# A two-layer block with a product-key expert choice on one core: which engine adds the candidate scores

## The chip, the cores and the metric

The kernel runs on one core of a Trainium2 chip. A core has five engines, each with its own queue of instructions: TensorE (PE in the rows; PEld is its weight load), VectorE (DVE), ScalarE (ACT), GpSimd (POOL) and SyncE (SP), which here only issues DMAs. The engines wait for each other by semaphores. The metric is the time of one execution in microseconds of device time, as the median of several runs. A profiled execution gives the start and the length of each instruction.

## The reference, cut to what matters

The program computes two transformer blocks over 512 tokens of width 1024, in float32. The second ends in `peer`: for each token and each of 8 heads two lists of 128 key scores are made, the best 16 of either list are taken, all sums of one of the first and one of the second list are formed, and the best 16 sums name 16 of 16,384 experts.

```python
def chunk(xc):
    q = (xc @ wq).reshape(PEER_CHUNK, PEER_HEADS, 2, half)
    s1 = jnp.einsum('chd,hnd->chn', q[:, :, 0], keys1).astype(jnp.float32)
    s2 = jnp.einsum('chd,hnd->chn', q[:, :, 1], keys2).astype(jnp.float32)
    v1, i1 = lax.top_k(s1, PEER_TOPK)
    v2, i2 = lax.top_k(s2, PEER_TOPK)
    cand = (v1[..., :, None] + v2[..., None, :]).reshape(PEER_CHUNK, PEER_HEADS, PEER_TOPK * PEER_TOPK)
    cidx = (i1[..., :, None] * PEER_N_KEYS + i2[..., None, :]).reshape(PEER_CHUNK, PEER_HEADS, PEER_TOPK * PEER_TOPK)
    best, pos = lax.top_k(cand, PEER_TOPK)
    eidx = jnp.take_along_axis(cidx, pos, axis=-1)
    g = jax.nn.softmax(best, axis=-1)
    a = jnp.einsum('chkd,cd->chk', u_tab[eidx], xc)
    wgt = (jax.nn.gelu(a.astype(jnp.float32)) * g).astype(xc.dtype)
    return jnp.einsum('chk,chkd->cd', wgt, v_tab[eidx])
```

## The kernel before

The first block, its mixture of experts and the second block's attention and convolution run up to about 1370 us. Then `peer` (L1395) begins. Its 512 tokens are four tiles of 128. Three tiles get their experts by dense products over the whole tables, with a weight of nought for what wasn't chosen; the fourth gathers its rows one by one with indirect DMAs. `peer` has three stages: the key choice (about 1380 to 1629 us), the making of the weight matrix from the choice (`gs`, to about 1930 us), and the products with the second table.

**The key choice** is a loop over 8 heads (L1604 to L1611). In each round the scores of the next head are made first and the present head's choice after them:

- `scores(h)` (L1522), for either half: a weight of 512 KB is loaded (`wraw`) and split into an upper part `whi` by ScalarE (L69) and a lower part `wlo` by GpSimd (L70); TensorE makes 24 products of 512 columns in three kinds (L87 to L89) into a bank `acc`; ScalarE copies it to `pq` (L1534); TensorE multiplies it with the keys (L1538); ScalarE copies the scores to `sk` (L1540). VectorE's `top16` (L1385) then takes the best 16 of each of the four tiles: a search for 8 values (L1388), their places (L1389), a copy without them (L1391), a second search (L1392) and its places (L1393), into `tkv` and `tki`.
- `best16(h)` (L1546): four instructions (L1551) add the two lists into `cand`, 80 sums per tile, those of the 256 that can be among the best 16. Three of them write 64 elements per partition, one 128. VectorE's `top16` looks for the best 16 sums (`best`, `pos`). ScalarE makes exponentials of them (`gslot`, L1565, with a load of its table in front). VectorE computes from `pos` which entries of the two lists make a sum (L1576 to L1582); ScalarE casts the result (`pu`, L1587), and VectorE looks the key numbers up (`eq`, L1590 to L1597, and `e`, L1598). ScalarE copies them to `slot` (L1599) and `ei` (L1602).

Beside it runs work of the later stages. `ahead` (L1436) makes chunks of the dense first product, each with a weight of its own (`whi`, `wlo`, 24 products of 384 columns, a gelu into `ga` at L1430, which needs another table in ScalarE): one after each half, one more in odd heads. `gather(2)` (L1478) starts two indirect DMAs of GpSimd in each head from head 1 on (`grow`, L1493); from head 2 on it multiplies a row gathered earlier with the token (L1503, GpSimd), and ScalarE sums it up (L1504).

**What sets the order.** The program is built under a scheduler that reorders the instructions of an engine by times of its own, within their dependencies. GpSimd is taken out of that from L1474 on: there its order is that of the code. So a head of GpSimd's queue is: four or five `wlo`, the four sums, the row products. TensorE, VectorE, ScalarE and SyncE are in the scheduler's order. TensorE has two `acc` banks and starts a group when ScalarE has copied the group before the last.

In `best16`, `tt` is VectorE's `tensor_tensor` (L1398). The blocks of the sums are (first place in `cand`, first entry of list one, its entries, entries of list two):

```python
BLOCKS = ((0, 0, 2, 16), (32, 2, 2, 8), (48, 4, 4, 4), (64, 8, 8, 2))
```

Of the kernel before, what the change touches and what calls it, by code (L numbers as in the profile page):

```python
# [46 lines left out]
class Emit:  # L47
# [1347 lines left out]
    def peer(self):  # L1395
        tc, nc, A = self.tc, self.nc, self.A
        mm = nc.tensor.matmul
        tt, ts, stt = nc.vector.tensor_tensor, nc.vector.tensor_scalar, nc.vector.scalar_tensor_tensor  # L1398
# [6 lines left out]
        with ExitStack() as es:  # L1405
# [30 lines left out]
            def ahead(n, eng=nc.gpsimd):  # L1436
                for _ in range(n):
                    if nu[0] < AHEAD:
                        u_chunk(nu[0], eng)
                        nu[0] += 1  # L1440
# [73 lines left out]
            with ExitStack() as ek:  # L1514
# [31 lines left out]
                def best16(h, val, ixu):  # L1546


                    cand = pk.tile([128, NT, 80], F32, name="cand")
                    for o, i0, ni, nj in BLOCKS:  # L1550
                        nc.gpsimd.tensor_tensor(  # L1551
                            cand[:, :, o:o + ni * nj].rearrange("p t (i j) -> p t i j", i=ni),
                            val[:, :, 0, i0:i0 + ni, None].to_broadcast([128, NT, ni, nj]),
                            val[:, :, 1, None, 0:nj].to_broadcast([128, NT, ni, nj]), op=ALU.add)
                    best = pk.tile([128, NT, 16], F32, name="best")
                    pos = pk.tile([128, NT, 16], U32, name="pos")
                    for t in range(NT):
                        self.top16(pk, cand[:, t], 80, best[:, t], pos[:, t])
                    ahead(h % 2)
                    g = pk.tile([128, NT, 16], F32, name="gslot")  # L1560
                    mx = pk.tile([128, NT], F32, name="bmx")
                    nm = pk.tile([128, NT], F32, name="bnm")
                    nc.scalar.activation(nm, best[:, :, 0], AF.Copy, scale=-1.0)
                    for t in range(NT):
                        nc.scalar.activation(g[:, t], best[:, t], AF.Exp, bias=nm[:, t:t + 1],  # L1565
                                             accum_out=mx[:, t:t + 1])
                    nc.vector.reciprocal(mx, mx)
                    hs = slice(h * 16, h * 16 + 16)
                    tt(slot[:, 2, :, hs], g[:, :ND], mx[:, :ND, None].to_broadcast([128, ND, 16]), op=ALU.mult)
                    tt(gg[:, hs], g[:, ND], mx[:, ND:NT].to_broadcast([128, 16]), op=ALU.mult)  # L1570
                    kf = pk.tile([128, NT, 2, 16], F16, name="kfl")
                    nc.scalar.activation(kf, ixu, AF.Copy)


                    u = [pk.tile([128, NT, 16], U32, name=f"pu{i}", bufs=1) for i in range(3)]
                    ts(u[0], pos, 2, 0x3c, op0=ALU.logical_shift_left, op1=ALU.bitwise_and)  # L1576
                    ts(u[0], u[0], 0x40, None, op0=ALU.bitwise_or)
                    ts(u[1], pos, 4, 7, op0=ALU.logical_shift_right, op1=ALU.bitwise_xor)
                    tt(u[2], u[0], u[1], op=ALU.logical_shift_right)
                    tt(u[1], u[2], u[1], op=ALU.logical_shift_left)  # L1580
                    tt(u[0], u[0], u[1], op=ALU.bitwise_xor)
                    ts(u[0], u[0], 0x3c, None, op0=ALU.bitwise_and)  # L1582
                    e = pk.tile([128, 2, NT, 16], F32, name="e12")
                    for half in range(2):

                        pu = pk.tile([128, NT * 16, 2], F16, name=f"pu2{half}")
                        nc.scalar.activation(pu, (u[0] if half else u[2]).rearrange("p t k -> p (t k)")[:, :, None]  # L1587
                                             .to_broadcast([128, NT * 16, 2]), AF.Copy)
                        eq = pk.tile([128, NT * 16, 16], F16, name="eq", bufs=2)
                        tt(eq.rearrange("p n (i j) -> p n i j", j=2), pu[:, :, None].to_broadcast([128, NT * 16, 8, 2]),  # L1590
                           i16[:, half].rearrange("p (i j) -> p i j", j=2)[:, None].to_broadcast([128, NT * 16, 8, 2]),
                           op=ALU.is_equal)
                        eq4 = eq.rearrange("p (t k) i -> p t k i", t=NT)
                        tt(eq4, eq4, kf[:, :, half, None, :].to_broadcast([128, NT, 16, 16]), op=ALU.mult)

                        for n in (8, 4):
                            tt(eq[:, :, 0:n], eq[:, :, 0:n], eq[:, :, n:2 * n], op=ALU.add)  # L1597
                        red(e[:, half].rearrange("p t k -> p (t k)"), eq[:, :, 0:4], axis=AX.X, op=ALU.add)  # L1598
                    nc.scalar.activation(slot[:, 0:2, :, hs], e[:, :, :ND], AF.Copy)  # L1599
                    ef = pk.tile([128, 16], F32, name="ef")  # L1600
                    stt(ef, e[:, 0, ND], 128.0, e[:, 1, ND], op0=ALU.mult, op1=ALU.add)
                    nc.scalar.activation(ei[:, hs], ef, AF.Copy)  # L1602

                cur = scores(0)  # L1604
                for h in range(8):
                    nxt = scores(h + 1) if h < 7 else None
                    if h == 7:
                        ahead(TRANS)
                    best16(h, *cur)
                    if h:  # L1610
                        gather(2)  # L1611
                    cur = nxt
# [334 lines left out]
```

## Time and profile before

| | us |
|---|---|
| median of three runs (2703.55 to 2711.38) | 2710.67 |
| profiled execution, its own time | 2710.84 |
| its span, first to last instruction | 2709.1 |
| TensorE busy in the span | 2445.6 (90%) |
| VectorE busy | 1824.4 (67%) |
| ScalarE busy | 1090.5 (40%) |
| GpSimd busy | 939.3 (35%) |
| key choice, from the sums of head 0 to behind those of head 7 | 223.5 |

Times in rows are microseconds from the start of the span. An instruction's row has its start, its length, engine, line, operation, what it writes and reads, and in square brackets how long the engine was idle before it and what ended that. Shares over the whole span mix stages that have different limits; the key choice is a twelfth of the span and is read by itself below.

### The profile page before, as it was taken

Reading aid. Unit: us, or ns where it says so; the run is one execution under the profiler, and the core shown is the slowest. Engines: PE = TensorE matmul, PEld = TensorE weight load, DVE = VectorE, ACT = ScalarE, POOL = GpSimd, SP = SyncE. Lnnn points to the kernel's source line nnn. Section 1 sums busy time; section 2 is a strip of 40 time slices with the busy share of each in tenths; the row PEclk is TensorE's granted clock in tenths of the full one; section 3 lists DMA queues with packets and bytes.
Section 4 is the critical chain, followed back from the end, with each engine's and each line's share of the span. In section 5 each row is a group of like instructions: output and inputs, shape, how many; then the busy total and the mean of one; then the engine's idle time right before and its main releaser. Section 6 shows DMA issues by size and latency. Waiting matters only on the chain.

```text
span 2709.1 us, 33479 instructions
## 1 busy us (share of the span) xinstructions
PE 2445.6 (90%) x11725; PEld 1911.1 (71%) x11725; DVE 1824.4 (67%) x3149; ACT 1090.5 (40%) x1688; POOL 939.3 (35%) x777
## 2 busy tenths in 40 slices
PE   7999897879977988989798889989899999999997
PEld 6776566423335766668587778979688878888886
DVE  6677965334346576564648889977877767767676
ACT  5555434212215336653444554434433333333233
POOL 1002640111100310000145665420676765666661
PEclk9999998889988988999899999989899999999998
DMA  4114684789975211104534448997699988888884
GB/s 143 63 56 170 226 291 159 283 336 391 400 274 212 94 59 47 39 31 144 186 114 136 148 159 305 348 347 276 197 299 301 305 299 266 291 300 284 275 294 152
DMA packets 215934, 589.47 MB, mean 218 GB/s; under 512 B 30565, under 2 KB 85349, under 8 KB 214740
## 3 DMA queue, kind: packets, MB, share of 16 engines
q1 hardware_dynamic: 170836, 433.91, 45.9%
q0 software_dynamic: 44928, 153.42, 16.1%
q8 instruction: 92, 1.51, 0.2%
q14 instruction: 78, 0.64, 0.1%
HBM read 541.85 MB, written 53.78 MB: 220 GB/s over the span
## 4 chain that ended last, share of the span: by engine, by line
PE 30%; DVE 12%; DMA 10%; issue 9%; ACT 4%; POOL 3%; POOLq 0%; SPq 0%; DVEq 0%; ACTq 0%
DMA wraw<-puT 5%; PE acc L87 4%; PE acc L89 4%; PE acc L88 4%; PE yp L87 4%; PE yp L88 4%; PE yp L89 4%; DMA grow<-pvr,ei 3%; POOL grow L1493 2%; DVE wlo L70 2%; DMA gd<-gs 1%; PE bank L87 1%; PE bank L89 1%; PE bank L88 1%; DVE gy L1510 1%
## 5 line engine op out<-in xcount | busy, mean ns | idle before, releaser
L69 ACT ACTIVATE whi<-wraw 128x1024 fp32r<-128x1024 f32 (+1 forms) x290 | 300.0, 1035 | 478.1 <-PE acc L88 164.2
L87 PE MATMUL acc<-hph,whi 128*128 128x384 f32 (+1 forms) x1152 | 404.3, 351 | 20.8 <-ACT ga L1430 19.9
L89 PE MATMUL acc<-hph,wlo 128*128 128x384 f32 (+1 forms) x1152 | 402.6, 350 | 6.5 <-DVE wlo L70 5.6
L88 PE MATMUL acc<-hpl,whi 128*128 128x384 f32 (+1 forms) x1152 | 399.4, 347 | 0.0
L70 DVE TENSOR_TENSOR wlo<-wraw,whi 128x1024 fp32r<-128x1024 f32 (+1 forms) x242 | 294.9, 1220 | 138.4 <-ACT whi L69 136.5
L70 POOL TENSOR_TENSOR wlo<-wraw,whi 128x1024 fp32r<-128x1024 f32 x48 | 115.7, 2416 | 481.4 <-ACT whi L69 468.2
L87 PE MATMUL yp<-vhi,wah 128*128 128x512 f32 x732 | 231.0, 395 | 17.4 <-ACT wah L69 17.4
L87 PEld LDWEIGHTS acc<-hph,whi 128*128 128x128 f32 x1152 | 220.5, 191 | 32.8 <-ACT ga L1430 24.6
L89 PEld LDWEIGHTS acc<-hph,wlo 128*128 128x128 f32 x1152 | 220.2, 191 | 19.5 <-DVE wlo L70 12.1
L88 PE MATMUL yp<-vlo,wah 128*128 128x512 f32 x732 | 231.1, 395 | 0.0
L89 PE MATMUL yp<-vhi,wal 128*128 128x512 f32 x732 | 228.3, 395 | 0.0
L88 PEld LDWEIGHTS acc<-hpl,whi 128*128 128x128 f32 x1152 | 220.5, 191 | 7.1 <-DVE hpl L70 0.2
L1685 POOL TENSOR_TENSOR gw<-gw,ga 128x256 f32<-128x256 f32 x128 | 175.8, 1374 | 137.9 <-DMA ga<-ad 76.7
L1493 POOL DMA_INDIRECT grow<-pu,ei x128 | 151.0, 1179 | 209.4 <-DVE grow L1506 173.3
L70 DVE TENSOR_TENSOR vlo<-wraw,vhi 128x1024 fp32r<-128x1024 f32 x122 | 157.6, 1292 | 93.5 <-ACT vhi L69 93.5
L1493 POOL DMA_INDIRECT grow<-pvr,ei x128 | 177.0, 1383 | 119.4 <-DVE gy L1510 96.3
L69 ACT ACTIVATE wah<-gw 128x384 fp32r<-128x384 f32 x126 | 66.2, 526 | 276.7 <-POOL gw L1686 223.3
L1510 DVE SCALAR_TENSOR_TENSOR gy<-grow,wt,gy 128x1024 f32<-128x1024 f32 x127 | 164.0, 1291 | 16.2 <-DMA grow<-pvr,ei 14.2
L87 PEld LDWEIGHTS yp<-vhi,wah 128*128 128x128 f32 x732 | 139.8, 191 | 47.8 <-ACT wah L69 20.4
L70 DVE TENSOR_TENSOR wal<-gw,wah 128x384 fp32r<-128x384 f32 x126 | 94.1, 747 | 104.2 <-ACT wah L69 103.7
L89 PEld LDWEIGHTS yp<-vhi,wal 128*128 128x128 f32 x732 | 139.6, 191 | 31.1 <-DVE wal L70 1.8
L88 PEld LDWEIGHTS yp<-vlo,wah 128*128 128x128 f32 x732 | 139.6, 191 | 27.7
(671 smaller groups left out, 5154.6 us busy)
## 6 DMA issues: line engine op xcount, KB each, us to landing
wraw<-wgu SPq DMA_DIRECT2D x128, 512.0 KB
wraw<-puT SPq DMA_DIRECT2D x128, 512.0 KB
wraw<-pv SPq DMA_DIRECT2D x128, 512.0 KB
wraw<-wd SPq DMA_DIRECT2D x64, 512.0 KB
aw<-wada SPq DMA_DIRECT2D x48, 512.0 KB
gd<-gs SPq DMA_DIRECT2D x8, 2048.0 KB
gw<-gd SPq DMA_DIRECT2D x128, 128.0 KB
ad<-ga SPq DMA_DIRECT2D x80, 192.0 KB
```

The costliest lines, as they stand in the source:

```text
L69: nc.scalar.activation(hi, src, AF.Copy)
L70: (eng or nc.vector).tensor_tensor(lo, src, f32(hi), op=ALU.subtract)
L87: mm(ps, lhsT=wh, rhs=xh, start=first, stop=False)
L88: mm(ps, lhsT=wh, rhs=xl, start=False, stop=False)
L89: mm(ps, lhsT=wl, rhs=xh, start=False, stop=last)
L1493: nc.gpsimd.indirect_dma_start(out=r, out_offset=None, in_=A["pu" if i < 128 else "pvr"], in_offset=bass.IndirectOffsetOnAxis(ap=ei[:, s:s ...
L1510: stt(gy, r, wt[:, s:s + 1], gy, op0=ALU.mult, op1=ALU.add)
L1685: nc.gpsimd.tensor_tensor(gw[:, :TG], gw[:, :TG], g[:, :TG], op=ALU.mult)
```

## The change

The four sums of a head are issued on VectorE in place of GpSimd. The operation, its operands and its shapes stay.

```diff
                     cand = pk.tile([128, NT, 80], F32, name="cand")
                     for o, i0, ni, nj in BLOCKS:
-                        nc.gpsimd.tensor_tensor(
+                        tt(
                             cand[:, :, o:o + ni * nj].rearrange("p t (i j) -> p t i j", i=ni),
                             val[:, :, 0, i0:i0 + ni, None].to_broadcast([128, NT, ni, nj]),
                             val[:, :, 1, None, 0:nj].to_broadcast([128, NT, ni, nj]), op=ALU.add)
```

GpSimd's queue loses the sums and is otherwise the same. The scheduler makes the order of the other engines anew.

**VectorE, where the search of head 3 begins.** `tkv` and `tki` are the lists (here the last entries of head 3's second list, then the first list of head 4), `best` and `pos` the search. Before:

```order
L1391 MATCH_REPLACE mr_10605<-tkv,sk 128x128
L1392 MAX tkv<-mr_10599 128x8
L1392 MAX tkv<-mr_10605 128x8
L1393 MAX_INDEX tki<-tkv,mr_10599 128x8
L1393 MAX_INDEX tki<-tkv,mr_10605 128x8
L1388 MAX best<-cand 128x8 x4
L1389 MAX_INDEX pos<-best,cand 128x8
L1391 MATCH_REPLACE mr_10935<-best,cand 128x80
L1389 MAX_INDEX pos<-best,cand 128x8
L1391 MATCH_REPLACE mr_10941<-best,cand 128x80
L1389 MAX_INDEX pos<-best,cand 128x8 x2
L1392 MAX best<-mr_10935 128x8
```

The row after these is the first search for head 4's first list. And now, where the three small sums stand ten rows further up, behind the first search's places:

```order
L1391 MATCH_REPLACE mr_10605<-tkv,sk 128x128
L1392 MAX tkv<-mr_10599 128x8
L1392 MAX tkv<-mr_10605 128x8
L1393 MAX_INDEX tki<-tkv,mr_10599 128x8
L1393 MAX_INDEX tki<-tkv,mr_10605 128x8
L1551 TENSOR_TENSOR cand<-tkv 128x4x32
L1388 MAX best<-cand 128x8 x4
L1389 MAX_INDEX pos<-best,cand 128x8
L1391 MATCH_REPLACE mr_10935<-best,cand 128x80
L1389 MAX_INDEX pos<-best,cand 128x8
L1391 MATCH_REPLACE mr_10941<-best,cand 128x80
```

The wide sum came in between the list and the search.

**VectorE, where the search of head 3 ends** and the arithmetic on the places begins (`pu`; `bmx` are the sums of the exponentials). Before:

```order
L1393 MAX_INDEX pos<-best,mr_10953 128x8
L1392 MAX tkv<-mr_10784 128x8
L1392 MAX tkv<-mr_10790 128x8
L1576 TENSOR_SCALAR pu_11004<-pos 128x64
L1578 TENSOR_SCALAR pu_11005<-pos 128x64
L1393 MAX_INDEX tki<-tkv,mr_10784 128x8
L1393 MAX_INDEX tki<-tkv,mr_10790 128x8
L1577 TENSOR_SCALAR pu_11004<-pu_11004 128x64
L1567 RECIPROCAL bmx<-bmx 128x4
```

And now:

```order
L1393 MAX_INDEX pos<-best,mr_10947 128x8
L1393 MAX_INDEX pos<-best,mr_10953 128x8
L1576 TENSOR_SCALAR pu_11004<-pos 128x64
L1578 TENSOR_SCALAR pu_11005<-pos 128x64
L1567 RECIPROCAL bmx<-bmx 128x4
L1577 TENSOR_SCALAR pu_11004<-pu_11004 128x64
L1569 TENSOR_TENSOR slot<-gslot,bmx 128x3x16
L1570 TENSOR_TENSOR gg<-gslot,bmx 128x16
L1579 TENSOR_TENSOR pu_11006<-pu_11004,pu_11005 128x64
```

The searches for the next head's first list, which stood among the search and the arithmetic, are gone from there: they now come with and behind the lookups.

**ScalarE, around the slot copy of head 3.** `sk` is the second half's scores of head 4 in both. Before:

```order
L1430 ACTIVATE ga<-acc 128x384
L1504 ACTIVATE grow,at<-grow 128x1024
L1540 ACTIVATE sk<-bank 128x512
L1599 ACTIVATE slot<-e_11014 128x6x16
L1602 ACTIVATE ei<-ef 128x16
L69 ACTIVATE whi<-wraw 128x1024
L1430 ACTIVATE ga<-acc 128x384
L1572 ACTIVATE kfl<-tki 128x128
```

And now:

```order
L1534 ACTIVATE pq<-acc 128x512
L1504 ACTIVATE grow,at<-grow 128x1024
L1599 ACTIVATE slot<-e_11014 128x6x16
L1602 ACTIVATE ei<-ef 128x16
L69 ACTIVATE whi<-wraw 128x1024
L1430 ACTIVATE ga<-acc 128x384
L1504 ACTIVATE grow,at<-grow 128x1024
L1540 ACTIVATE sk<-bank 128x512
L69 ACTIVATE whi<-wraw 128x1024
L1430 ACTIVATE ga<-acc 128x384
L1572 ACTIVATE kfl<-tki 128x128
```

The second half's scores moved from ahead of the slot copy to five rows behind it.

## Rows read from the trace of the kernel before

**Rows 1.** Busy time by stretch, sum of the eight: length, each engine's busy time.
```profile
sum 223.52, PE 196.84 PEld 177.17 DVE 197.31 ACT 118.09 POOL 137.80; mean PE 24.61 PEld 22.15 DVE 24.66 ACT 14.76 POOL 17.22
```

**Rows 2.** Waits of 1390 to 1640 us: who waited for whom, total, times, longest.
```profile
ACT slot L1599 <- DVE e L1598: 33.3, 8, 6.0
DVE best L1388 <- POOL cand L1551: 27.6, 8, 4.9
...
DVE tkv L1388 <- ACT sk L1540: 5.8, 1, 5.8
```

**Rows 3.** Timeline of one wait for sums, VectorE's and GpSimd's rows.
```profile
1518.05 0.67 DVE L1388 MAX8 best<-cand 128x8 f32<-128x80 f32 x4 [4.92 <-POOL cand L1551]
...
1514.50 2.39 POOL L70 TENSOR_TENSOR wlo<-wraw,whi 128x1024 fp32r<-128x1024 f32 x1 [1.56 <-ACT whi L69]
1516.84 1.18 POOL L1551 TENSOR_TENSOR cand<-tkv 128x128 f32<-128x128 f32 x4
```

**Rows 4.** The sums by line (ns least/median/most, starts); a like VectorE group by shape.
```profile
L1551 POOL TENSOR_TENSOR cand<-tkv x32: 293/302/422, 1405.7 to 1602.2; 128x64 f32<-128x64 f32 x24, 128x128 f32<-128x128 f32 x8
...
L1580 DVE TENSOR_TENSOR pu<-pu,pu 128x64 uint32<-128x64 uint32 x8 | 1.8, 220 | 0.0
```

**Rows 5.** Groups by shape, 1395 to 1625 us (busy, mean ns | idle); two by line.
```profile
L1576 DVE TENSOR_SCALAR pu<-pos 128x64 uint32<-128x64 uint32 x8 | 26.9, 3368 | 0.0
L1594 DVE TENSOR_TENSOR eq<-eq,kfl 128x1024 f16<-128x1024 f16 x16 | 25.8, 1636 | 0.0
...
L1597 DVE TENSOR_TENSOR eq<-eq 128x512 f16<-128x512 f16 x16 | 12.6, 813 | 0.0
...
L1578 DVE TENSOR_SCALAR pu<-pos 128x64 uint32<-128x64 uint32 x8 | 1.4, 181 | 0.0
...
L1594 DVE TENSOR_TENSOR eq<-eq,kfl x16: 685/694/2887, 1419.0 to 1616.8; 128x1024 f16<-128x1024 f16 x16
...
L1597 DVE TENSOR_TENSOR eq<-eq x31: 270/404/3314, 1420.2 to 1618.9; 128x512 f16<-128x512 f16 x16, 128x256 f16<-128x256 f16 x15
```

**Rows 6.** Timeline, VectorE's long L1594 and GpSimd's instruction over it.
```profile
1503.77 2.85 DVE L1594 TENSOR_TENSOR eq<-eq,kfl 128x1024 f16<-128x1024 f16 x1
...
1503.47 2.60 POOL L70 TENSOR_TENSOR wlo<-wraw,whi 128x1024 fp32r<-128x1024 f32 x1 [3.29 <-issue]
```

**Rows 7.** Timeline: head 7's search and ScalarE behind it; the arithmetic of head 3.
```profile
1602.57 0.67 DVE L1388 MAX8 best<-cand 128x8 f32<-128x80 f32 x4 [0.77 <-POOL cand L1551]
...
1606.38 2.78 DVE L1576 TENSOR_SCALAR pu<-pos 128x64 uint32<-128x64 uint32 x1
...
1609.56 0.49 ACT L1430 ACTIVATE ga<-acc 128x384 f32<-128x384 f32 x1
...
1500.16 0.18 DVE L1578 TENSOR_SCALAR pu<-pos 128x64 uint32<-128x64 uint32 x1
...
1501.96 1.28 DVE L1590 TENSOR_TENSOR eq<-pu,i 128x1024 f16<-128x1024 f16 x2
```

**Rows 8.** Timeline of ScalarE in head 3.
```profile
1502.30 1.04 ACT L69 ACTIVATE whi<-wraw 128x1024 fp32r<-128x1024 f32 x1
...
1504.65 0.49 ACT L1430 ACTIVATE ga<-acc 128x384 f32<-128x384 f32 x1
1505.04 1.05 ACT L1504 ACTIVATE grow<-grow 128x1024 f32<-128x1024 f32 x1
...
1506.08 0.59 ACT L1540 ACTIVATE sk<-bank 128x512 f32<-128x512 f32 x1
1508.38 0.28 ACT L1599 ACTIVATE slot<-e 128x96 f32<-128x96 f32 x1 [1.72 <-DVE e L1598]
```

**Rows 9.** Timeline of VectorE in head 0, the second list's beginning.
```profile
1397.84 0.87 DVE L1388 MAX8 tkv<-sk 128x8 f32<-128x128 f32 x4 [5.77 <-ACT sk L1540]
...
1400.19 0.48 DVE L1392 MAX8 tkv<-mr 128x8 f32<-128x128 f32 x2
```

**Rows 10.** Stretch behind: instruction counts in brackets, then granted clock, DMA share, GB/s.
```profile
1660.00:1700.00 40.00, 39.84 (x275) 38.41 (x273) 38.75 (x68) 17.07 (x26) 20.63 (x15) 1.00 0.97 344
```

## The prediction, made before the changed kernel ran

> **What bounds the kernel now.** I read first the table of busy time by stretch, cut at the eight places where the sums are made, one head to a row, and its sum. The key choice takes eight such stretches, 223.5 us in all. TensorE is busy for 196.8 us of it and VectorE for 197.3 us [rows 1]: neither is full, and GpSimd (137.8) and ScalarE (118.1) are far from it. So the stage is paced by waits between engines, and the list of waits is the second view. Its third entry is the one that the change is about: VectorE waits for the sums eight times, 27.6 us together [rows 2]. Add that to VectorE's busy time and 224.9 us comes out, the whole of the stage: in this stage VectorE either works or waits for GpSimd's sums. It waits for its score tile (`sk`) only once, 5.8 us, at the first head [rows 2].
>
> The timeline of one such wait, the third view, tells why it is long. VectorE is through with its lists at 1513.1 (1518.05 less 4.92). GpSimd reaches the sums at 1516.84, because its order is written by hand and a weight's lower half (`wlo`, 2.39 us) stands ahead of them; the four sums take 1.18 us, and VectorE goes on at 1518.05 after 4.92 us [rows 3]. The sums proper are the small part of the wait; the queue in front of them is the large one.
>
> The fourth view is the groups of instructions by shape, for what VectorE calls busy there. The first index instruction (L1576) takes 3368 ns on the mean and its twin of the same shape (L1578) 181 ns; L1594 has a median of 694 ns, a least of 685 and a longest of 2887 [rows 5]. The long ones lie under a GpSimd instruction that works between tiles: an L1594 starts at 1503.77 and ends at 1506.62, GpSimd's `wlo` at 1506.07 [rows 6]. Some of VectorE's instructions stand still until GpSimd has ended. Against the undisturbed shape it costs over the eight heads 8 x 3.19 (L1576) + 16 x 0.94 (L1594) + 16 x 0.41 (wide L1597, 813 against the median of 404) = 25.5 + 15.1 + 6.5 = 47 us [rows 5].
>
> **The change part by part.** The profiled execution took 2710.84 us (span 2709.1 and 1.7 around it), 0.2 us above the median of the three runs; the sum is made against it.
>
> Removed: 27.6 us of waiting [rows 2]. GpSimd loses 32 sums of 302 ns [rows 4], about 10 us; with 86 us of the stage idle [rows 1] it is not the bound, so I give its shorter queue nothing.
>
> Added: 32 sums on VectorE. The nearest row is L1580, two SBUF operands of 64 elements: 220 ns [rows 4]. 24 sums have 64 elements, 8 have 128, for which I take 0.29: 24 x 0.22 + 8 x 0.29 = 7.6 us. Starts overlap a little (5 us is the low end); twice L1580 for the wide one gives 8.8 as the high end.
>
> Moved, and this is the larger part: the order of VectorE and ScalarE is made anew by the scheduler. Two covers go.
>
> First, the search. Today the next head's first list is built in between the search's instructions, so ScalarE's exponentials and index casts are ready when VectorE gets to them. In the new order nothing stands between. Head 7 is the row for that, since there is no next list there today either: the search begins at 1602.57 and is over at 1606.38, but ScalarE, behind the exponentials, a weight's upper half and a table load, is at its gelu only at 1609.56, and the index cast comes after it, at about 1610.05, ready at 1610.36 [rows 7]. That is 4.0 us behind the end of the search. The arithmetic that VectorE has for this gap, from L1578 to L1590 at 1500.16 to 1501.96, is 1.8 us [rows 7]. So about 2.2 us of idle time comes into each of heads 0 to 6, 7 x 2.2 = 15.4 us. Today head 7's gap is hidden by L1576, which waits for GpSimd anyway; so the ends are 0 and 7 x 4 = 28 us, and I take 15.4 because the new ScalarE order in four of these heads is that of head 7.
>
> Second, the second list. Its scores (`sk`) now stand in ScalarE's queue behind the slot copy, which waits for VectorE's last lookup, and behind a weight's upper half, a gelu and a row product. From rows: 1.04 (`whi`) + 0.39 (gelu, start to start) + 1.04 (row product) + 0.59 (`sk`) = 3.1 us, and about 0.3 for the slot copy [rows 8]. VectorE has the tail of the first list left in that time, about 1 us. So it waits some 2.4 us; for five heads (2 to 6) 12.0, for heads 0 and 1, whose chain has no row product, 1.4 each: 14.8 us. This is a wait that today's table has only at the start [rows 2]. Ends: nothing, and 7 x 3.4 = 24 us.
>
> The stalls against GpSimd: the search will now end while GpSimd has nothing to do, since its next `wlo` needs a `whi` that ScalarE makes behind the exponentials; so L1576's 25.5 us mostly go. But in the new order that `wlo`, and behind it a weight and two row products (2.4 us each), fall on the lookups (L1590 to L1597), where today they fall on L1576. One block costs 2887 - 685 = 2.2 us [rows 5]. I count three in each of heads 3, 5 and 7; two in heads 2, 4 and 6, where one product falls on the next list's searches, which read one tile and are as long as ever; one in heads 0 and 1, without products: 17 blocks, 37.4 us. And the sums themselves: two SBUF operands, as L1594 has. In the new order of each head a `whi` stands right behind the second `sk`; its `wlo` holds GpSimd from about 1.1 to 3.5 us after `sk`, and the three small sums come 2.4 us after it (four searches, then six index instructions: 1397.84 to 1400.19 [rows 9]). So they wait about 1.1 us in each of eight heads. Together 46.2, against 47 today: -0.8. Ends: half of it (-24), and every bundle of sums under a full block, 8 x 2 x 2.2 = 35 in place of 8.8 (+26).
>
> The rows show VectorE halted by GpSimd at L1594 [rows 5, 6]. The Trainium skill (SBUF — State Buffer, section Who interferes with whom) says that a VectorE instruction with two SBUF inputs and a GpSimd instruction that reads SBUF use one port, and that the second to begin stands still until the first has ended. It speaks against this change, for by it each sum can be halted; the trace agrees at L1594, and no run here shows a sum on VectorE. If it did not hold for the sums, 8.8 us would leave the total.
>
> Behind the stage the work is the same. From 1660 to 1700 TensorE is busy for 39.84 of 40 us and VectorE for 38.75 [rows 10], so a later start there ends later by as much. One weight's 24 products move from in front of the slot transposes to behind them, 4 us of TensorE's work; I give that nothing, with 4 us either way.
>
> The sum: -27.6 + 7.6 + 15.4 + 14.8 - 0.8 = **+9.4 us**, 2710.8 + 9.4 = 2720.2, so **2720 us**.
>
> **The rivals.** One: the wait goes and nothing takes its place. ScalarE gets ahead of VectorE, so that casts and scores lie ready; then -27.6 + 7.6 = -20.0, 2691 us. For it: VectorE waits for ScalarE only once today, and TensorE's 26.7 us of slack in the stage [rows 1] would allow it. Against it: the second `sk` stands behind the slot copy in the new order, and that copy needs VectorE's last lookup, so ScalarE cannot get ahead there; today it waits 33.3 us for that lookup [rows 2]. It decides where both covers together cost under a quarter of their 30 us.
>
> Two: the wait only changes its name. The two covers cost half (15 us) and the stalls stay at today's 47: -27.6 + 7.6 + 15 = -5, 2706 us. For it: all the engines are coupled in a ring here, and what one wait loses another takes. Against it: head 7's row has its 4 us without any ring.
>
> Three: the port to the letter. Both bundles of sums (three small, one wide) meet a full GpSimd instruction in each head, which adds 35 - 9 = 26 us: 2746 us. For it: GpSimd works 137.8 of 223.5 us [rows 1]. Against: ahead of the wide sum GpSimd has mostly run out of halves to make.
>
> That the sums don't land on VectorE is excluded by its order; that they stand late there is not: they follow the second list at once.
>
> **How the numbers follow.** A measurement of this kernel can tell about 0.3%, 8 us, from no change. The forecast has 0.50 and its own range is 2712 to 2734: 0.40 of it above 2719, slower, and 0.10 below, within. Rival three has 0.08, slower. Rival two 0.20, within. Rival one 0.22, faster. That makes 0.22 faster, 0.30 within, 0.48 slower. The predicted time is the forecast's, 2720. Both signs hold much of the chance, so the range takes in half of rival one and leaves out most of rival three: 2696 to 2738.
>
> **What would show it.** The waits of VectorE for GpSimd's sums are gone (certain). The list of waits has "VectorE `tkv` for ScalarE's `sk`" seven times or more, 10 to 24 us; if under 4 us, my second cover is wrong. VectorE waits for ScalarE's casts or exponentials, 10 to 28 us. L1576's mean falls below 1 us, and those of L1590, L1594 and L1597 rise; the three small sums of a head take well over 0.22 us at their first. The stretch from the first to the last sum, 1405.7 to 1602.2 today [rows 4], grows from 196.5 to between 200 and 215 us. A stretch under 190 us makes the prediction wrong whatever the terms; so does a gain or loss that arises behind 1640 us, where the work is only re-ordered.

## The result, and the profile after

The changed kernel takes 2721.5 us (median of five runs, 2720.6 to 2726.4) against 2709.1 for the kernel before beside it (five runs, 2702.0 to 2711.4): a ratio of 1.0052, 95% interval 1.0037 to 1.0066. So 12 us were lost, and the forecast was 2720. The total was met, by luck; the working behind it was not, and most of what follows is about that.

The first view to read is again the table by stretch. The first two rows are the key choice from VectorE's first search among sums to the slot transposes (TensorE turns the finished `slot` entries over), and all behind it; the last is the sum of eight stretches cut at the sums, as in [rows 1]. Columns: length, busy time of TensorE, its weight load, VectorE, ScalarE, GpSimd with the number of instructions, then TensorE's mean granted clock as a share of full speed, the DMA engines' busy share and GB/s.

```profile
1408.15:1644.08 235.93, 198.09 (x954) 179.07 (x952) 209.77 (x903) 113.30 (x239) 125.62 (x62) 0.90 0.40 129
1644.08:2721.20 1077.12, 1020.81 (x5476) 897.01 (x5474) 817.92 (x1052) 404.19 (x601) 591.26 (x502) 0.98 0.84 287
...
sum 242.98, PE 205.14 PEld 185.77 DVE 216.44 ACT 118.36 POOL 128.59; mean PE 25.64 PEld 23.22 DVE 27.05 ACT 14.79 POOL 16.07
```

The same two stretches of the kernel before:

```profile
1406.89:1623.34 216.45, 189.78 (x954) 170.10 (x952) 192.56 (x876) 111.78 (x236) 133.22 (x90) 0.95 0.45 147
1623.34:2709.10 1085.76, 1024.82 (x5452) 900.43 (x5452) 815.37 (x1052) 403.05 (x600) 588.86 (x500) 0.97 0.82 283
```

So the change lost **19.5 us in the key choice** and got **8.6 back behind it**; 1.3 lie ahead. VectorE's busy time in the key choice grew by 17.2 us (192.56 before), while the 28 sums in that stretch need only some 6.5 us undisturbed. TensorE's 954 products there took 8.3 us longer, at a mean granted clock of 0.90 in place of 0.95, and TensorE idled for 37.8 us in place of 26.7.

The list of waits of 1390 to 1645 us tells where the waiting went (compare [rows 2]).

```profile
POOL wlo L70 <- ACT whi L69: 85.6, 21, 8.7
ACT slot L1599 <- DVE e L1598: 62.4, 8, 9.7
DVE tkv L1388 <- ACT sk L1540: 34.3, 9, 14.1
...
DVE bmx L1567 <- ACT gslot L1565: 9.8, 8, 3.9
```

The wait for the sums is gone. In its place VectorE waits for scores: 34.3 us, of which the longest (14.1) and one of 5.78 at 1402.74 lie ahead of the first search, so 14.4 in seven waits belong to the second lists. It waits 9.8 us for the exponentials. Together 24.2 us: the wait nearly kept its size and got two new names.

The groups of VectorE by shape, 1395 to 1645 us (busy, mean ns | idle), answer [rows 4, 5]:

```profile
L1594 DVE TENSOR_TENSOR eq<-eq,kfl 128x1024 f16<-128x1024 f16 x16 | 32.7, 2066 | 0.0
...
L1590 DVE TENSOR_TENSOR eq<-pu,i 128x1024 f16<-128x1024 f16 x16 | 21.4, 1352 | 0.0
...
L1582 DVE TENSOR_SCALAR pu<-pu 128x64 uint32<-128x64 uint32 x8 | 15.6, 1948 | 0.1
L1597 DVE TENSOR_TENSOR eq<-eq 128x512 f16<-128x512 f16 x16 | 13.8, 875 | 0.0
...
L1551 DVE TENSOR_TENSOR cand<-tkv 128x64 f32<-128x64 f32 x24 | 8.8, 419 | 0.0
...
L1551 DVE TENSOR_TENSOR cand<-tkv 128x128 f32<-128x128 f32 x8 | 2.1, 269 | 0.0
L1576 DVE TENSOR_SCALAR pu<-pos 128x64 uint32<-128x64 uint32 x8 | 2.1, 260 | 0.3
```

L1576, at 3368 ns before, is short. But L1582, the last of the index instructions, is long (1948 ns; 0.19 undisturbed), L1590 has doubled (685 before) and L1594 grew by 430 ns. Against their undisturbed rows the excess is 14.1 (L1582) + 10.7 (L1590: 16 x 0.67) + 22.2 (L1594: 16 x 1.386) + 7.5 (L1597: 16 x 0.47) and 3.5 in the sums, 58 us. This excess is called a stall below: the instruction counts as busy, but stands still. With the same arithmetic the kernel before has 47, and 3 more in L1579, which the prediction left out.

One head shows how it comes about, head 4 in the timeline. VectorE's rows:

```profile
1522.09 1.43 DVE L1551 TENSOR_TENSOR cand<-tkv 128x64 f32<-128x64 f32 x3
...
1532.27 0.18 DVE L1567 RECIPROCAL bmx<-bmx 128x4 f32<-128x4 f32 x1 [1.17 <-ACT gslot L1565]
1532.37 1.29 DVE L1582 TENSOR_SCALAR pu<-pu 128x64 uint32<-128x64 uint32 x1
...
1533.79 3.94 DVE L1590 TENSOR_TENSOR eq<-pu,i 128x1024 f16<-128x1024 f16 x2
1537.65 6.25 DVE L1594 TENSOR_TENSOR eq<-eq,kfl 128x1024 f16<-128x1024 f16 x2
```

GpSimd's rows of the same time:

```profile
1520.77 2.39 POOL L70 TENSOR_TENSOR wlo<-wraw,whi 128x1024 fp32r<-128x1024 f32 x1 [0.46 <-ACT whi L69]
1531.26 2.36 POOL L70 TENSOR_TENSOR wlo<-wraw,whi 128x1024 fp32r<-128x1024 f32 x1 [8.09 <-ACT whi L69]
1533.75 0.98 POOL L1493 DMA_INDIRECT grow<-pu,ei  x1
1534.74 2.42 POOL L1503 TENSOR_TENSOR grow<-grow,htok 128x1024 f32<-128x1024 f32 x1
1537.32 1.26 POOL L1493 DMA_INDIRECT grow<-pu,ei  x1 [0.16 <-issue]
1538.60 2.40 POOL L1503 TENSOR_TENSOR grow<-grow,htok 128x1024 f32<-128x1024 f32 x1
1540.95 2.40 POOL L70 TENSOR_TENSOR wlo<-wraw,whi 128x1024 fp32r<-128x1024 f32 x1
```

Read them against each other. The first of the three sums (1522.09 to 1523.52 together) stands still until the `wlo` of 1520.77 ends at 1523.16. L1582 ends at 1533.66, just behind the `wlo` of 1531.26. The second L1590 ends behind the product of 1534.74. The pair of L1594 lasts 6.25 us in place of 1.29 and is over at 1543.90, because a product and a `wlo` follow each other without a gap. GpSimd idled for 8.09 us, most of it while VectorE searched, where it would have halted nothing, and worked almost without a break while VectorE did the lookups.

### The profile page after: what moved, and what is told of

It is laid out like the page before. It is cut to its first block, busy times and chain, and to the rows that moved or that the text cites. A ratio compares the mean times of both kernels' runs of the same rounds, so it can differ in the third digit from the quotient of the medians.

```text
span 2721.2 us, 33475 instructions
## 1 busy us (share of the span) xinstructions
PE 2450.0 (90%) x11725; PEld 1916.5 (70%) x11725; DVE 1843.8 (68%) x3181; ACT 1091.0 (40%) x1690; POOL 931.0 (34%) x745
## 4 chain that ended last, share of the span: by engine, by line
PE 51%; DVE 17%; DMA 14%; issue 9%; ACT 6%; POOL 2%; SPq 0%; DVEq 0%; ACTq 0%; POOLq 0%
PE acc L87 7%; PE acc L88 7%; PE acc L89 7%; DMA wraw<-puT 5%; PE yp L87 4%; PE bank L658 4%; PE yp L88 4%; PE yp L89 4%; DVE wlo L70 2%; PE bank L87 2%; DMA grow<-pvr,ei 2%; PE bank L88 2%; PE bank L89 2%; DMA aw<-wada 2%; DVE gy L1510 1%
## 5 line engine op out<-in xcount | busy, mean ns | idle before, releaser
L87 PE MATMUL yp<-vhi,wah 128*128 128x512 f32 x732 | 228.5, 392 | 15.8 <-ACT wah L69 15.8
L1510 DVE SCALAR_TENSOR_TENSOR gy<-grow,wt,gy 128x1024 f32<-128x1024 f32 x127 | 163.7, 1289 | 12.3 <-DMA grow<-pvr,ei 10.3
```

The source lines that it names most:

```text
L87: mm(ps, lhsT=wh, rhs=xh, start=first, stop=False)
L1510: stt(gy, r, wt[:, s:s + 1], gy, op0=ALU.mult, op1=ALU.add)
```

## The experiments

Each kernel ran beside the kernel before on the same chip; ratios are to that. "Key choice" in the table is the time from VectorE's first search among sums (head 0) to its last instruction on the places (head 7). The columns after it split that time, from the start of one VectorE instruction to the start of the next, as read from each timeline; stalls are inside "arithmetic, lookups, rest". The searches take 96 to 98 us in all of them (91.5 in the one by hand) and are left out. Each row is one profiled execution, and the cut begins behind the sums of head 0.

| kernel | ratio (95%) | key choice | waits for GpSimd | waits for ScalarE | sums | arithmetic, lookups, rest |
|---|---|---|---|---|---|---|
| before | 1 | 216.1 | 23.3 | 0 | 0 | 97.1 |
| after | 1.0052 (1.0037 to 1.0066) | 233.8 | 0 | 24.2 | 9.9 | 102.7 |
| token | 1.0000 (0.9986 to 1.0015) | 216.2 | 16.8 | 0 | 11.6 | 91.9 |
| early | 1.0088 (1.0057 to 1.0119) | 225.4 | 5.4 | 15.8 | 0 | 106.6 |
| oldorder | 1.0038 (1.0022 to 1.0055) | 228.0 | 0 | 12.0 | 10.3 | 109.7 |
| slotdve | 1.0143 (1.0108 to 1.0178) | 248.1 | 0 | 9.5 | 6.6 | 135.5 |
| hand | 1.0117 (1.0080 to 1.0154) | 246.5 | 0 | 32.0 | 6.8 | 116.1 |
| noprod_b | 0.9933 (0.9915 to 0.9952) | 202.7 | 19.9 | 4.8 | 0 | 81.7 |
| noprod | 0.9955 (0.9939 to 0.9971) | 207.7 | 0 | 23.3 | 12.6 | 74.5 |
| gpool0_b | 0.9965 (0.9953 to 0.9976) | 216.0 | 9.1 | 5.5, and 3.0 for gathered rows | 0 | 101.9 |
| gpool0_a | 0.9984 (0.9966 to 1.0001) | 224.0 | 0 | 11.1 | 12.4 | 103.8 |
| late_b | 0.9885 (0.9861 to 0.9908) | 209.9 | 24.1 | 1.3 | 0 | 88.6 |
| late_a | 0.9895 (0.9877 to 0.9913) | 204.3 | 0 | 20.6 | 12.3 | 74.4 |
| late_old | 0.9875 (0.9854 to 0.9895) | 209.6 | 0 | 13.7 | 10.3 | 89.6 |

### The engine or the order: token and early

In **token** the sums are VectorE's, but behind a mark that GpSimd makes where its sums stood.

```diff
                     cand = pk.tile([128, NT, 80], F32, name="cand")
+                    nc.gpsimd.memset(cand[:, 0, 0:80:16], 0.0)
                     for o, i0, ni, nj in BLOCKS:
```

> The sums are VectorE's, but a small GpSimd write of five elements of the sums' tile stands where GpSimd's sums stood, so the sums wait for GpSimd's queue as before, and the scheduler's order is that of before (the next head's first list within the search, the second list's scores ahead of the slot copy). Theory one, the order is what costs (the two covers 24 us, and stalls that grew by 9): VectorE's wait for GpSimd stays 22 to 28 us, the waits for scores and exponentials stay under 6 us together, L1576 is long again; 2704 to 2714 us, the kernel before within 0.2%. Theory two, VectorE as the sums' engine is what costs (their own time and their stalls): 2718 us or more.

It took 2711.5 us, before 2712.0. Its row of the list of waits, and of the groups by shape:

```profile
DVE cand L1552 <- POOL cand L1550: 19.9, 7, 3.8
```

```profile
L1577 DVE TENSOR_SCALAR pu<-pos 128x64 uint32<-128x64 uint32 x8 | 14.4, 1801 | 0.0
...
L1570 DVE TENSOR_TENSOR slot<-gslot,bmx 128x48 f32<-128x48 f32 x8 | 8.8, 1104 | 0.0
L1552 DVE TENSOR_TENSOR cand<-tkv 128x128 f32<-128x128 f32 x8 | 8.8, 1098 | 19.9 <-POOL cand L1550 19.9
...
L1552 DVE TENSOR_TENSOR cand<-tkv 128x64 f32<-128x64 f32 x24 | 3.9, 217 | 0.0
```

(Its lines are one higher: L1577 is L1576 of before.) The time is theory one's: with GpSimd's place in the order kept, VectorE as the engine of the sums costs nothing that can be measured. The wait was to be 22 to 28 us and was 19.9, and L1577 is long in four heads only; in the other four a halt of 1.8 us fell on L1570, a little behind it in VectorE's order (2.0 us in place of 0.2). The sums' 11.6 us, 6.6 of them a stall of the wide sum, are paid by a wait 6.5 us shorter and by a last column 5 us shorter.

In **early** the sums stay on GpSimd, one weight further up in its queue.

```diff
                             self.top16(pk, sk[:, t], 128, val[:, t, half], ixu[:, t, half])
+                        if half == 1 and prev:
+                            cand = sums(prev[0])
                         ahead(1)
...
```

> The sums are GpSimd's as before, but stand one weight further up in its queue, ahead of the chunk that follows the second list; by the scheduler's order the search then has no list within it and the second scores stand behind the slot copy, as in the changed kernel. Theory one, order: the wait for the sums falls from 27.6 to 10 to 16 us (four sums and the way there and back), and both covers go as in the changed kernel, 20 to 28 us of waits for scores and exponentials; 2712 to 2726 us. Theory two, engine: the wait falls and nothing else costs, 2692 to 2700 us.

It took 2732.0, more than before, more than the changed kernel, and more than either theory. The wait for sums fell further than expected, and the waits for scores and exponentials, without head 0's 5.8, came to 15.8 us where theory one had 20 to 28:

```profile
DVE tkv L1388 <- ACT sk L1540: 14.6, 8, 5.8
...
DVE bmx L1572 <- ACT gslot L1570: 7.0, 6, 3.9
...
DVE best L1388 <- POOL cand L1551: 6.1, 8, 0.8
```

So a wait of 27.6 us was cut to 6 without moving anything to VectorE, and 0.9% was lost. Of that 9 us are in the key choice; behind the transposes this run was 7 us longer than the profile of before, and TensorE was busy there for 1032.1 us in place of 1024.8. ScalarE's gelus tell why: 19 chunks of the dense first product were made in the key choice in place of 22, so three more, each of 24 products of 0.17 us, were left for the part behind. The key choices of these kernels don't hold quite the same work.

### The covers: slotdve, hand, oldorder

**slotdve** takes the copies that wait for the last lookup out of ScalarE's queue.

```diff
-                    nc.scalar.activation(slot[:, 0:2, :, hs], e[:, :, :ND], AF.Copy)
+                    nc.vector.tensor_copy(slot[:, 0:2, :, hs], e[:, :, :ND])
...
-                    nc.scalar.activation(ei[:, hs], ef, AF.Copy)
+                    nc.vector.tensor_copy(ei[:, hs], ef)
```

> The changed kernel with the copies into slot and ei made by VectorE, so that ScalarE no longer waits for the lookups there. If the second cover is what it seems (scores stand behind a copy that waits for the last lookup): the waits of the second list for sk fall from 14.4 to under 4 us, VectorE gets 16 short copies (3 to 4 us), the stage shortens by 6 to 12 us; 2709 to 2717 us. If the scores are late for another reason (TensorE or the weight's upper half): the wait stays above 10 us, 2721 to 2726 us.

2751.1 us, the worst of all and outside either expectation. The waits for scores did vanish:

```profile
ACT kfl L1572 <- DVE tki L1393: 66.9, 7, 12.8
...
DVE bmx L1567 <- ACT gslot L1565: 9.5, 8, 3.9
...
DVE tkv L1388 <- ACT sk L1540: 5.8, 1, 5.8
```

The one left is that of the first head. VectorE was also later here, so this run alone doesn't show that the slot copy had held the scores up; the changed kernel's own trace does. There TensorE's products for the second list's scores ended 4.0, 6.4, 8.9 and 9.0 us ahead of ScalarE's copy in heads 1, 2, 4 and 6 (in head 4 at 1510.17, while ScalarE waited for the lookups until 1516.17 and copied the scores at 1519.11); in heads 3, 5 and 7 the copy to `pq`, which those products need, itself stood behind the slot copy. So the second cover's mechanism is as predicted. But its removal bought nothing: ScalarE now waits 66.9 us at the next place that needs VectorE, the cast of the key numbers (`kfl`), and the lookups and the rest take 135.5 us in place of 102.7. VectorE's waits fell by 14.7 us; of the 33 that came, 8 are the 16 copies and the others stalls.

**hand** has VectorE's order in the key choice written out: sums, search, arithmetic, the next head's second list, lookups, the first list of the head after.

```diff
+                        b = best16(cur)
+                        next(b)
+                        if h < 7:
+                            scores(nxt, 1)
+                        next(b, None)
...
+                        if h < 6:
+                            nxt = lists(h + 2)
+                            scores(nxt, 0)
```

> The sums are VectorE's and VectorE's order in the key choice is written by hand: sums and search of a head, arithmetic on the places, the next head's second list, lookups, the first list of the head after. Both covers are there by construction, and no wait for GpSimd. Theory one, order: no wait for sums, those for scores and exponentials under 8 us together, stalls against GpSimd 40 to 60 us as in both kernels; from the first sums to the slot transposes 198 to 210 us (217.6 before, 239.0 in the changed kernel); 2692 to 2706 us. Theory two, engine: 2715 us or more. Rival to both: TensorE, with 190 us of work in the stage, or ScalarE becomes the bound: 2706 to 2712 us with new waits for sk.

2740.3 us. That lies in theory two's range, but not by its reason, since the sums take 6.8 us here; the rival had the new waits for scores, but a time 28 us too short. VectorE waits 35.1 us for scores, and TensorE 37.6 us for banks, as the list of waits has it:

```profile
PE acc L87 <- ACT ga L1430: 37.6, 10, 6.2
DVE tkv L1525 <- ACT sk L1555: 35.1, 11, 5.8
```

It was an order of my own, and says only that a cover in VectorE's order is no cover where ScalarE's order, made by the scheduler, delivers late.

**oldorder** is the test of the prediction's main claim. VectorE's order is that of the kernel before, by hand, and the sums wait for nothing.

```diff
+PAT1 = ((11, 1), (4, 0), (2, 1), (6, 0), (2, 1), (2, 0), (2, 1), (2, 0), (2, 1), (2, 0), (1, 1), (2, 0), (2, 1), (2, 0))
+PAT2 = ((14, 1), (4, 0), (2, 1), (6, 0), (2, 1), (2, 0), (2, 1), (8, 0))
...
+                        for n, it in PAT1:
+                            go(b if it else l, n)
```

(`b` gives the instructions of the present head's choice, `l` those of the next head's list.)

> VectorE's order of the kernel before, written out by hand (11 instructions of the search, then the next head's first list within the rest of it, the second list within the lookups), but the sums are VectorE's own and wait for nothing. This is the change without the new order. Theory one, each term by itself: the wait (23 to 28 us) goes, the sums cost 7 to 10, the covers are there, the stalls against GpSimd stay at some 48 us; from the first search to the slot transposes 196 to 204 us (216.4 before), 2692 to 2702 us. Theory two, the ring: VectorE is then early at the arithmetic and the lookups, while GpSimd works at the pace that ScalarE's upper halves set, so that the stalls grow and waits for sk come, by what the wait gave: 212 to 222 us, 2706 to 2720 us.

2721.7 us, as the changed kernel, and 228.3 us to the transposes. Theory one, mine, falls; theory two has the mechanism, and its ranges were too low by 6 and 2 us. The two rows that decide, from the list of waits and from the groups by shape:

```profile
DVE tkv L1529 <- ACT sk L1559: 12.0, 7, 3.0
```

```profile
L1587 DVE TENSOR_SCALAR pu<-pos 128x64 uint32<-128x64 uint32 x8 | 34.9, 4367 | 0.0
```

L1587 is L1576 of before. In token, with nearly the same order of VectorE's and a wait of 16.8 us, it took 1801 ns; without the wait it takes 4367, 20.5 us more in eight heads. Some of that is a stall that token has at L1570. Over all instructions the table's last column rose by 17.8 us; with 12.0 us of waits for scores that is 30 us for the 16.8 that were taken out, and the key choice grew by 11.8 us. One reservation: the pair doesn't differ in the wait alone. ScalarE's order was left to the scheduler (the four exponentials stand together), L1570 stands further back, and in the odd heads the second list begins four lookups earlier than in token.

### GpSimd's work beside the lookups: noprod, gpool0 and late

**noprod** (from the changed kernel) and **noprod_b** (from the kernel before) leave out one line.

```diff
                     if i < GPOOL:
-                        nc.gpsimd.tensor_tensor(r, r, ht, op=ALU.mult)
                         nc.scalar.activation(r, r, AF.Copy, accum_out=at[:, s:s + 1])
```

> The changed kernel without GpSimd's products of the gathered rows with the tokens (that part of the computation is left out; the gathers and ScalarE's row sums stay): 14 instructions of 2.42 us go from GpSimd's queue in the key choice. If VectorE's stalls come from GpSimd's work on SBUF in whatever place it falls: of 58 us of stalls (L1582 14, L1590 11, L1594 22, L1597 8, sums 3) 12 to 25 go, and the stage shortens by as much, 2700 to 2712 us. If the long instructions come from elsewhere, or the lower halves slide into the freed time: 2718 to 2726 us.

> The kernel before without the same products (left out as there). By the stall theory: 48 us of stalls fall by 8 to 16, but the wait for the sums, whose queue is shorter too, falls by at most some us; 2692 to 2704 us. If VectorE's wait for sums takes what the stalls give (GpSimd's weights set the pace): 2706 to 2713 us.

2698.4 and 2693.4 us: 23 less than the changed kernel and 16 less than before. These two don't compute the whole result and stand only for their times. In noprod the groups shrink as they should (lines are one lower: L1593 is L1594):

```profile
L1593 DVE TENSOR_TENSOR eq<-eq,kfl 128x1024 f16<-128x1024 f16 x16 | 18.5, 1173 | 0.0
L1589 DVE TENSOR_TENSOR eq<-pu,i 128x1024 f16<-128x1024 f16 x16 | 13.6, 863 | 0.0
L1581 DVE TENSOR_SCALAR pu<-pu 128x64 uint32<-128x64 uint32 x8 | 13.2, 1650 | 0.1
L1596 DVE TENSOR_TENSOR eq<-eq 128x512 f16<-128x512 f16 x16 | 10.6, 677 | 0.0
```

L1594 gave 14.2 of its 22.2 us of stalls and L1590 7.8 of 10.7: the products were most of what halted them. L1582 stayed long (1650 ns), under a `wlo`. The waits for scores and exponentials stayed (23.3 us). Without the products the key choices of the two kernels are 5.0 us apart (207.7 and 202.7), with them 17.7.

**late_b**, **late_a** and **late_old** compute everything, but gather no rows in the key choice (from before, after and oldorder); VectorE multiplies them later.

```diff
-                    if h:
-                        gather(2)
...
-GPOOL = 16
+GPOOL = 0
```

> The kernel before (sums on GpSimd) with no gathered rows in the key choice: the 14 gathers and their products come behind it, where VectorE multiplies (VectorE 70% busy, the DMA engines 82%, in the second table's part). Nothing is left out. If GpSimd's products halt VectorE in the key choice and nothing else, the gain of the run without products (16 us) stays and the 14 rows behind cost 0 to 8: 2692 to 2704 us. If the rows behind cost what they save (DMA share there): 2705 to 2715.

> The changed kernel (sums on VectorE) in the same way. By the stalls: the run without products was at 2698, so 2697 to 2709, and no faster than late_b, since both covers are still gone (23 us of waits for scores and exponentials) and a wait of 20 to 24 us for sums is what late_b has in their place. If the new order is worse than the old by itself: 8 us or more behind late_b.

> VectorE's order of the kernel before by hand, sums on VectorE without a wait, and no gathered rows in the key choice. If the stalls under GpSimd's products were what took the 20 us of the removed wait: now it shows, the stage is 8 to 20 us shorter than that of late_b, 2680 to 2694 us. If weights' halves alone set VectorE back (each wlo under the lookups, and scores that come late): as late_b within 5 us.

2678.6, 2679.2 and 2675.0 us, all about 1.1% faster than before, faster than expected, and within 0.2% of each other: here the time doesn't tell which engine makes the sums, in which order, or with which wait. For late_old that answers its question against the products: its key choice is as long as late_b's (209.6 and 209.9), though a wait of 24.1 us is gone. In its place stand 12.4 us more of waits for scores, the sums' 10.3, and 1.0 in the last column. So in the old order the wait bought nothing even without GpSimd's products. All three beat both kernels, and by more than the runs without products. Yet of late_b's gain only 3.6 us are in the key choice (216.4 to 212.8, to the transposes); 34 are behind it, and 7 were lost ahead of it. Behind it the row of the table by stretch is

```profile
1626.86:2678.80 1051.94, 1003.80 (x5405) 884.94 (x5403) 823.52 (x1067) 395.00 (x587) 589.25 (x503) 0.98 0.85 295
```

The rows that moved there cost nothing that can be seen; VectorE has 8 us more to do. TensorE's busy time is 21 us shorter than in the kernel before and its idle time 13 us shorter. Two chunks more were made in the key choice (24 in place of 22), which is 8 of the 21; the rest is open. It is not a matter of VectorE's stalls in the key choice.

**gpool0_b** and **gpool0_a** split that: the gathers stay in place, only the products are VectorE's.

```diff
-GPOOL = 16
+GPOOL = 0
```

> The kernel before, with its gathers where they are, but the products of the gathered rows made by VectorE (1.22 us each, with the row sum in the same instruction) in place of GpSimd (2.42 us) and ScalarE. If what helped the kernels with late rows is that GpSimd no longer works over VectorE's lookups: some 15 us of stalls go and 17 us of products come, so the stage is 210 to 220 us as before, and 2700 to 2712 us; the later place of the rows is then worth the rest. If it is the rows' place that hardly matters and the engine all: 2676 to 2690 us.

> The changed kernel in the same way. Without GpSimd's products its stalls fall by some 25 us and 17 us of products come on VectorE, partly into its 24 us of waits for scores and exponentials: 2698 to 2712 us, and within 6 us of the kernel before made the same way, since it is GpSimd's products that made the sums' new place cost. If the new order costs by itself: 8 us or more behind it.

2701.5 and 2709.2 us against 2710.6. The engine of the products is worth 9 us in the kernel before, the place of the rows some 22 more (2701.5 to 2678.6). None of the 9 us is in the key choice, 216.0 us in place of 216.1, though three chunks more were made in it. gpool0_a is level with before and 8 us behind gpool0_b, between the 6 and the 8 that were to decide. So with GpSimd's products away by one means or another the changed kernel is behind by 5, 8 or 0.6 us. By the means of the runs that is 4.5, 7.4 and 0.5 us, each with a 95% interval of some 5 or 6 us either way, against 12 with the products: the loss is smaller without them, and in gpool0 not gone. The key choices alone are 5.0 and 8.0 us longer, and in late_a 5.6 shorter. In gpool0_b a trade can be seen again: 25 us of products came onto VectorE, the wait for sums fell by 14, and the stage stayed at 216.

## Why the prediction was right in its total and wrong in its working

**The wait of 27.6 us goes: right.** No row of it is left.

**The sums, 7.6 us, and 8.8 of stalls at them: too dear.** They took 9.9 us in the account by starts, which leaves out head 0, and 10.9 by the groups; 24 x 0.217 + 8 x 0.269 = 7.4 of that undisturbed, 3.5 stalled. The bundle met a `wlo` in four heads, not in eight.

**The first cover, 15.4 us: 9.8, and in another place.** Heads 0 to 6 have 0.65 to 1.17 us each (5.9), and head 7, which I counted as nothing, 3.92. The gap was to be a wait for the cast; no such wait is in the list, since L1582, in front of the lookups, stood still for 14.1 us, the first cast was made meanwhile (in head 4 at 1532.15, with L1582 from 1532.37 to 1533.66), and the second, at 1533.70, under the first lookup. VectorE waited for the exponentials instead.

**The second cover, 14.8 us: right in size and mechanism.** 14.4 us in seven waits, with the scores' products ready and ScalarE's copy late behind the slot copy.

**The stalls at the arithmetic and lookups, 37.4 against today's 47: this step failed.** They became 54.5 (58 less the sums'). I had L1576's stall go, as it did, and three blocks of 2.2 us in the later heads. I left out L1582 altogether, which took 14.1, since I listed L1590 to L1597 as what a halt can hit; and I priced a block as one GpSimd instruction, where GpSimd's often come in pairs, as at 1538.60 and 1540.95. The rows for either stood ahead of the prediction: L1576 is of L1582's kind, and its mean of 3368 ns [rows 5] is more than one `wlo` of 2.39.

**Behind the stage 0 (4 either way): -8.6.** By the prediction's own test this speaks against the working, as does the stretch from the first to the last sum, 1405.1 to 1622.85 = 217.8 us in place of 200 to 215. With the measured terms my sum is -27.6 + 7.4 + 9.8 + 14.4 + 8 (58 against 50) = +12.0. The key choice lost 19.5 between the cuts of the table: head 0's wait of 4.3 us lies ahead of them, the searches took 1.4 more, and 1.8 more passed between the last lookup and the transposes. The part behind gave back what made the total fit: that is luck. TensorE's products there took 4.0 us less, though a chunk's 24 came in addition, at a granted clock of 0.98 in place of 0.97, and it idled 4.6 us less; the prediction has no term for either. Token, whose program is nearly that of before, took 1080.5 us behind the transposes and 1085.8 was before's, so some 5 of the 8.6 us may be what two executions differ by anyway; the cause is open.

**Rivals.** Rival two, the wait only changes its name, is what the waits did (23.3 to 24.2 in the account) and what oldorder and early show again: three kernels that cut the wait, on either engine and in either order, have a key choice of 225 to 234 us (slotdve and hand, with more changes, 247 and 248), and the two that have it 216. Its price was wrong, because it took the covers at 15 us, which cost 24, and the stalls as fixed, which grew by 8. Rival one, that nothing takes the wait's place, fails on the same 24 us; rival three, 35 us of stalls at the sums, on 3.5. My forecast's reason, that the new order is what costs, holds no further than the waits; with the old order waits and stalls took as much.

What ties this together, as far as it is shown: in this stage VectorE's time is its work, its waits, and its stalls under GpSimd, and the last two trade in these kernels. The sums were made on GpSimd behind its `wlo`, so VectorE waited where it would else have gone into arithmetic that GpSimd halts. That the wait lined VectorE up with GpSimd's pauses is read from token and oldorder (91.9 and 109.7 us in the last column); that it is the cause is argued, since no run moved the wait alone. That GpSimd's products over the lookups make most of the change's loss in the key choice is shown by the pair without them, 5.0 us in place of 17.7; leaving them out also shortens GpSimd's queue, and no run tells the two apart. That they are the whole of it isn't shown: gpool0 keeps 8 us, and late_old gained nothing from the removed wait without them. Nor has any run set apart TensorE's lower clock in the changed key choice.

## What to carry to other kernels

A wait for a slow engine may cover the time in which that engine would otherwise stall the waiting one; before it is removed, look at what the waiting engine does next and whether the other is then at work. A stalled instruction counts as busy, so compare the mean of each shape with its least: here some 50 us of VectorE's "busy" time in the key choice were stalls before the change. And split a gain by stage before giving it a cause: moving the gathered rows out of that stretch made the kernel 1.1% faster, but nearly all of it came behind the stretch, for reasons that are mostly open.

## What the runs showed of the hardware

A VectorE instruction that GpSimd had halted was not let in between two GpSimd instructions that followed without a gap: the longest L1594 of the changed kernel took 5662 ns where 0.68 is its own, over a product and a `wlo` of 2.40 us each. The Trainium skill (SBUF — State Buffer, section Who interferes with whom) has the second to begin blocked until the other's instruction is over, by which one block here would be 2.4 us at most, one GpSimd instruction of the trace. The trace agrees for single instructions (the second L1590 of head 4: 3.94 for the pair, 1.29 undisturbed), and for pairs the measured 5 us decides.

Nor do the starts in the rows tell who goes first: in head 4 the second L1590 begins at about 1534.4 and the second L1594 at 1538.25, each some 0.35 us ahead of GpSimd's product, and both stood still until it was over. GpSimd's starts in the profile are rough, so this may be the record and not the chip.

The searches, which read one tile of scores or sums, are as long with GpSimd's products in the stage as without them: 95.7 us in the kernel before, 96.1 in noprod_b. L1576 and L1582 read one tile as well, and are halted (3368 and 1948 ns on the mean, about 190 undisturbed).
